# Score products of heads of 64 columns: two products on stacked rows in place of three on half rows

## The chip, the cores and the metric

The program runs on one core of one Trainium2 chip. The metric is the device time of one execution in microseconds (us). Before the change three executions took 1540.32, 1541.56 and 1544.6 us; the median, 1541.56 us, is the time before.

## The reference, cut to what matters

Two transformer blocks are computed for 256 tokens of width 1024 in fp32. The first block (latent attention, then grouped attention, each with a gated feed-forward part) isn't touched. The second block has a mixer between two feed-forward parts, and in it two kinds of attention whose heads have 64 columns:

```python
DA_HEADS = 8; DA_HEAD_DIM = 64          # differential attention: 8 heads, each of 2 components c
s = jnp.einsum('bqhcd,bkhcd->bhcqk', qblk, k) * scale
p = jax.nn.softmax(s, axis=-1)
a = p[:, :, 0] - lam * p[:, :, 1]
...
DIL_HEADS = 12; DIL_HEAD_DIM = 64       # 3 dilation groups of 4 heads each
s = jnp.einsum('nbqhd,nbkhd->nbhqk', qb, kc) * scale
s = jnp.where(valid, s, NEG)
```

A score matrix of one head component is 256 queries x 256 keys, a sum over 64 columns.

## The kernel before, in words

**Number format.** TensorE multiplies values of a rounded fp32 type (`fp32r`). To keep the accuracy of fp32, every operand is split (`split`, line 670): `hi` is the value rounded by ScalarE (`ACTIVATE`, Copy), `lo` is the value less `hi`, by VectorE (`TENSOR_TENSOR`, subtract). `mm3` (line 621) multiplies two split operands with three products into one place in PSUM: hi by hi, hi by lo, lo by hi. A product is one weight load (the queries, 128 columns) and one matmul (the keys, 256 columns).

**The mixer of the second block** (`mixer2`, line 1696). The first loop has four steps b, each with two heads. A step projects queries and keys to tokens x columns (`tm`), rotates them (`rope2`) and transposes them with TensorE into two PSUM tiles of 128 x 512: rows are head columns (component c has rows 64c to 64c+63), and the 512 columns are two heads of 256 tokens. `split` writes each PSUM tile to an `act` tile of [128, 2, 512]: plane 0 is hi, plane 1 is lo. For each head, component c and block j of 128 queries, `mm3` works on the 64 rows of the component, so on rows 0 to 63 or on rows 64 to 127: 4 x 2 x 2 x 2 = 32 scores of 128 queries, 96 products. VectorE takes the maximum, ScalarE the exponential, VectorE combines the two components, TensorE transposes the result (`pt`) and multiplies it by the values (`o`).

The second loop has two steps b for the dilated heads: three PSUM tiles pA, pB, pC (queries of groups 0 and 1, keys of groups 0 and 1, queries and keys of group 2) are split to three `act` tiles; for each slot sl (rows 64 sl on), group g and block j there is one `mm3`: 2 x 2 x 3 x 2 = 24 scores, 72 products. A fused VectorE instruction adds the mask and finds the maximum (`sm`).

**What sets the order.** No instruction runs where it is written. `record` (line 210) collects all operations, and `schedule` (line 319) orders each engine's list: six rounds of a forward pass (line 397) and a backward pass that gives each operation a latest start as its priority; the best round is kept. On TensorE the planner prices a product of `fp32r` by its output columns, whatever its rows, and knows one change of form only, that to and from outputs of 32 rows:

```python
if op.kw["lhsT"].root.dtype == F32R:
    return n / 2.4 + 13.3
```

Products into the same PSUM tile keep their written order; products of different tiles may be mixed, and projections of later steps (`tm`, `gate`) are put between them. All `act` tiles share 34 slots of SBUF, the split weights (`whi`, `wlo`) among them. The chip follows these fixed lists; each engine works through its own in order.

Of the kernel before, what the change touches and what calls it, by code (L numbers as in the profile page):

```python
# [9 lines left out]
F32 = mybir.dt.float32  # L10
F32R = mybir.dt.float32r
I32 = mybir.dt.int32
AF = mybir.ActivationFunctionType
ALU = mybir.AluOpType
# [3 lines left out]
P = 128  # L18
D = 1024
T = 256  # L20
# [526 lines left out]
class Net:  # L547
# [104 lines left out]
    def fold(self, ps, s="fold"):  # L652

        t = self.tmp(512, s)[:64]
        self.nc.scalar.activation(t, ps[64:], AF.Copy)
        self.nc.vector.tensor_tensor(t, t, ps[:64], op=ALU.add)
        return t

    def both(self, tiles, k):

        return tiles[k // 2][:, :, (k % 2) * T:(k % 2 + 1) * T]
# [1034 lines left out]
    def mixer2(self, a, rm):  # L1696
        nc = self.nc
# [16 lines left out]
        for b in range(4):  # L1714
            w = self.halves("win2a", b // 2 * 3 + b % 2)
            pts = [self.ps("qkT") for _ in range(2)]
            for j in range(2):
                ps = self.tok512(a, j, w)
                x = self.tmp(512, "qk")
                for t in range(2):  # L1720
                    nc.scalar.activation(x[:, t * T:(t + 1) * T], ps[:, t * T:(t + 1) * T], AF.Copy, scale=rqk(t, j))
                self.rope2(x, j, 8)
                for t in range(2):
                    for hd in range(2):
                        c = t * T + hd * P
                        nc.tensor.transpose(pts[t][:, hd * T + j * P:hd * T + (j + 1) * P], x[:, c:c + P], self.ident)
            qkT = []
            for pt in pts:
                o = self.act("qkT")
                self.split((o[:, 0], o[:, 1]), pt)  # L1730
                qkT.append(o)
            qT, kT = qkT
            if b % 2 == 0:
                w = self.halves("win2a", b // 2 * 3 + 2)
                vs = []
                for j in range(2):
                    o = self.act("v")
                    self.split((o[:, 0], o[:, 1]), self.tok512(a, j, w), scale=rqk(1, j))
                    vs.append(o)
            po = self.ps("o")  # L1740
            for hd in range(2):
                es = []
                for c in range(2):
                    pscore = self.ps("s")
                    c0 = c * 64
                    for j in range(2):
                        q0 = hd * T + j * P
                        self.mm3(pscore[:, j * T:(j + 1) * T],
                                 (qT[c0:c0 + 64, 0, q0:q0 + P], qT[c0:c0 + 64, 1, q0:q0 + P]),
                                 (kT[c0:c0 + 64, 0, hd * T:(hd + 1) * T], kT[c0:c0 + 64, 1, hd * T:(hd + 1) * T]),  # L1750
                                 True, True)
                    m = self.small(2)
                    nc.vector.tensor_reduce(m, pscore.rearrange("p (j n) -> p j n", j=2), axis=AX.X, op=ALU.max,
                                            negate=True)
                    e = self.tmp(512, "e")
                    l = self.small(2)
                    for j in range(2):
                        nc.scalar.activation(e[:, j * T:(j + 1) * T], pscore[:, j * T:(j + 1) * T], AF.Exp,
                                             bias=m[:, j:j + 1], accum_out=l[:, j:j + 1])
                    r = self.small(2)  # L1760
                    nc.vector.reciprocal(r, l)
                    nc.vector.tensor_scalar(r, r, (self.sig, self.siglam)[c], None, op0=ALU.mult)
                    es.append((e, r))
                (e0, r0), (e1, r1) = es
                aa = []
                for j in range(2):
                    s = slice(j * T, (j + 1) * T)
                    self.times("vector", e1[:, s], r1[:, j:j + 1])
                    nc.vector.scalar_tensor_tensor(e0[:, s], e0[:, s], r0[:, j:j + 1], e1[:, s], op0=ALU.mult,
                                                   op1=ALU.subtract)  # L1770
                    aa.append(e0[:, s])
                pT = self.transposed(aa, 2)[0]
                for c in range(2):
                    v0 = b % 2 * T + hd * P
                    self.mm3(po[:, hd * T:(hd + 1) * T], self.hl(vs[c], v0, v0 + P),
                             self.hl(pT, c * T, (c + 1) * T), c == 0, c == 1)
            os_ = self.tmp(512, "os")
            nc.scalar.activation(os_, po, AF.Copy)
            sq = self.tmp(512, "sq")
            nc.scalar.activation(sq, po, AF.Square)  # L1780
            ss = self.colsum(sq, 4)
            v = self.small(4)
            nc.vector.tensor_scalar(v, ss, 1.0 / P, self.epss, op0=ALU.mult, op1=ALU.add)
            nc.vector.tensor_scalar(v, v, 1e-37, None, op0=ALU.max)
            fit = self.small(4)
            nc.vector.tensor_scalar(fit, ss, self.ovs, self.ovt, op0=ALU.mult, op1=ALU.is_lt)
            r = self.pow_half(v, 4)
            nc.vector.tensor_tensor(r, r, fit, op=ALU.mult)
            rb = self.rows(r, 4)
            t = self.tmp(512, "on")  # L1790
            nc.vector.scalar_tensor_tensor(t, os_, self.gsub, rb, op0=ALU.mult, op1=ALU.mult)
            o = self.act("oa")
            self.split((o[:, 0], o[:, 1]), t)
            oa.append(o)
# [8 lines left out]
        for b in range(2):  # L1803
            xs, va = {}, []
            pA, pB, pC = self.ps("qT"), self.ps("kT"), self.ps("qkT")
            where = {(0, 0): (pA, 0), (0, 1): (pA, T), (0, 2): (pC, 0),
                     (1, 0): (pB, 0), (1, 1): (pB, T), (1, 2): (pC, T)}
            for t in range(2):
                w = [self.weights("win2d", (b * 3 + t) * 2 + i, 1536, 384) for i in range(2)]
                for j in range(2):  # L1810
                    ps = prod(j, w, 384)
                    x = self.tmp(384, "qk")
                    nc.scalar.activation(x, ps, AF.Copy, scale=rqk(t, j))
                    self.rope2(x, j, 6)
                    for g in range(3):
                        d, o = where[t, g]
                        nc.tensor.transpose(d[:, o + j * P:o + (j + 1) * P], x[:, g * P:(g + 1) * P], self.ident)
            tt = {}
            for p in (pA, pB, pC):
                o = self.act("qkT")  # L1820
                self.split((o[:, 0], o[:, 1]), p)
                tt[id(p)] = o
            w = [self.weights("win2d", (b * 3 + 2) * 2 + i, 1536, 384) for i in range(2)]
            for j in range(2):
                ps = prod(j, w, 384)
                o = self.act("v")
# [1 line left out]
                va.append(o)  # L1828
            po = self.ps("o")
            for sl in range(2):  # L1830
                r0 = sl * 64
                sms = [self.actf("sm")[:, :768] for _ in range(2)]
                mx = self.small(6)
                for g in range(3):
                    qd, qo = where[0, g]
                    kd, ko = where[1, g]
                    q, kk = tt[id(qd)], tt[id(kd)]
                    pscore = self.ps("s")
                    for j in range(2):
                        self.mm3(pscore[:, j * T:(j + 1) * T],  # L1840
                                 self.hl(q[r0:r0 + 64], qo + j * P, qo + (j + 1) * P),
                                 self.hl(kk[r0:r0 + 64], ko, ko + T), True, True)
                    for j in range(2):
                        nc.vector.tensor_tensor_reduce(sms[j][:, g * T:(g + 1) * T], pscore[:, j * T:(j + 1) * T],
                                                       mask[g][:, j], 1.0, NEG * 4, ALU.add, ALU.max,
                                                       mx[:, j * 3 + g:j * 3 + g + 1])
                m = self.small(2)
                nc.vector.tensor_reduce(m, mx.rearrange("p (j g) -> p j g", j=2), axis=AX.X, op=ALU.max, negate=True)
                l, r = self.small(2), self.small(2)
# [6 lines left out]
                for c in range(6):  # L1856
                    g, kc = divmod(c, 2)
# [10 lines left out]
        for i in range(8):  # L1868
            w = self.weights("win2g", i, 2048)
            g = self.gate_tile(i)  # L1870
            for mm in range(2):
                ps = self.ps("gate")
# [240 lines left out]
```

## Time and profile before

| what | value |
|---|---|
| median of three executions | 1541.56 us |
| the profiled execution | 1544.4 us, its span 1542.4 us |
| TensorE matmul (PE) | 1514.7 us busy, 98% of the span, 8808 products |
| TensorE weight load (PEld) | 1307.8 us, 85% |
| VectorE (DVE) | 1129.6 us, 73% |
| ScalarE (ACT) | 831.6 us, 54% |
| GpSimd (POOL) | 96.9 us, 6% |
| mean granted TensorE clock | 0.994 |

The profile is one execution on the chip. Busy times of matmuls include the tail of each product, so that neighbours overlap: what a product costs TensorE is read from the distance between the starts of two neighbours, not from its own duration. All operations have line 543, the line that issues the planned lists, so they are told apart by tile names: `tm` projection, `s` score, `qkT`, `qT`, `kT` transposes of queries and keys and their split, `pt` and `pT` transposed probabilities, `o` output. The two loops of the mixer lie between about 1096 and 1250 us of the span.

### The profile page before, as it was taken

The page shows a single profiled execution, that of the slowest core. Times are in us where ns is not written, and L with a number is a line of the kernel's source. Part 1 is how long each engine was busy: PE and PEld are TensorE (multiplying, and loading weights), DVE is VectorE, ACT ScalarE, POOL GpSimd, SP SyncE. Part 2 cuts the span into 40 slices and gives each one's busy share as a digit, 9 for nine tenths or more (in the row PEclk, how much of TensorE's full clock was granted, in tenths as well). Part 3 has the DMA queues.
Part 4 walks back from the last instruction along what each step waited for, and adds up shares of the span by engine and source line. Part 5 has one row for each costly group of instructions (what it writes and reads, how often), then busy time and mean ns, then how long its engine had stood idle before and what let it go on. Part 6 is the DMA issues. An engine that isn't in the chain of part 4 may idle for free.

```text
span 1542.4 us, 22782 instructions
## 1 busy us (share of the span) xinstructions
PE 1514.7 (98%) x8808; PEld 1307.8 (85%) x8808; DVE 1129.6 (73%) x2075; ACT 831.6 (54%) x1525; POOL 96.9 (6%) x109
## 2 busy tenths in 40 slices
PE   8989999999999999999999999999999999999998
PEld 6877788888788889998888888888889999888886
DVE  6478988649935757889977676765877887787752
ACT  4358944322431344786866565554756666575540
POOL 1120000000000000200000011100100000111100
PEclk8999999999999999999999999999999999999999
DMA  9355353326815731325645464454522444564450
GB/s 369 132 203 197 114 200 123 136 83 245 301 55 184 266 123 56 110 83 183 231 161 198 161 242 164 157 213 177 192 89 98 153 172 173 191 219 164 164 191 28
DMA packets 40940, 258.30 MB, mean 167 GB/s; under 512 B 4864, under 2 KB 5120, under 8 KB 14848
## 3 DMA queue, kind: packets, MB, share of 16 engines
q1 hardware_dynamic: 40832, 256.85, 46.5%
q8 instruction: 69, 1.13, 0.3%
q14 instruction: 39, 0.32, 0.1%
HBM read 255.78 MB, written 1.05 MB: 167 GB/s over the span
## 4 chain that ended last, share of the span: by engine, by line
PE 84%; DVE 7%; ACT 3%; DMA 3%; issue 2%; POOL 0%; SPq 0%; DVEq 0%; POOLq 0%; ACTq 0%
PE u L543 19%; PE g L543 19%; PE dn L543 11%; PE tm L543 10%; PE y L543 8%; PE gate L543 3%; PE s L543 2%; DVE wlo L543 2%; PE o L543 2%; PE pa L543 1%; PE p L543 1%; PE mod L543 1%; PE pt L543 1%; DVE X L543 1%; ACT whi L543 1%
## 5 line engine op out<-in xcount | busy, mean ns | idle before, releaser
L543 ACT ACTIVATE whi<-raw 128x1024 fp32r<-128x1024 f32 (+3 forms) x393 | 395.5, 1026 | 244.8 <-DMA raw<-wup 64.7
L543 DVE TENSOR_TENSOR wlo<-raw,whi 128x1024 fp32r<-128x1024 f32 (+3 forms) x393 | 458.7, 1184 | 81.6 <-PE dn L543 25.0
L543 PE MATMUL dn<-mid,whi 128*128 128x512 f32 (+1 forms) x576 | 173.4, 375 | 0.0
L543 PE MATMUL g<-h,whi 128*128 128x512 f32 (+1 forms) x528 | 170.5, 389 | 1.6 <-ACT h L543 1.1
L543 PE MATMUL u<-h,whi 128*128 128x512 f32 (+1 forms) x528 | 169.9, 388 | 0.0
L543 PE MATMUL dn<-mid,wlo 128*128 128x256 f32 (+1 forms) x376 | 122.2, 325 | 0.0
L543 PEld LDWEIGHTS dn<-mid,whi 128*128 128x128 f32 x576 | 105.2, 189 | 19.9
L543 PE MATMUL g<-a,whi 128*128 128x512 f32 x336 | 119.9, 396 | 0.4 <-DVE a L543 0.4
L543 PE MATMUL u<-a,whi 128*128 128x512 f32 x336 | 119.5, 395 | 0.0
L543 PEld LDWEIGHTS g<-h,whi 128*128 128x128 f32 x528 | 99.3, 189 | 22.2 <-ACT h L543 1.4
L543 PEld LDWEIGHTS u<-h,whi 128*128 128x128 f32 x528 | 99.6, 190 | 20.7 <-issue 0.4
L543 PE MATMUL tm<-whi,a 128*128 128x512 f32 (+1 forms) x384 | 116.5, 372 | 0.0
L543 PE MATMUL u<-h,wlo 128*128 128x256 f32 (+1 forms) x344 | 115.7, 336 | 0.0
L543 PE MATMUL g<-h,wlo 128*128 128x256 f32 (+1 forms) x344 | 115.3, 335 | 0.0
L543 PE MATMUL y<-whi,mid 128*128 128x512 f32 x352 | 109.1, 390 | 0.0
L543 PE MATMUL g<-a,wlo 128*128 128x256 f32 x336 | 94.8, 282 | 0.0
L543 PE MATMUL u<-a,wlo 128*128 128x256 f32 x336 | 94.4, 281 | 0.0
L543 POOL TENSOR_TENSOR small<-small,mhalf 128x2 f32<-128x2 f32 (+2 forms) x34 | 37.6, 1108 | 890.1 <-DVE small L543 884.4
L543 DVE SCALAR_TENSOR_TENSOR macc<-raw,sc,macc 128x1024 f32<-128x1024 f32 x70 | 86.7, 1281 | 4.8 <-DMA raw<-wmod 4.5
L543 PEld LDWEIGHTS y<-whi,mid 128*128 128x128 f32 x352 | 66.1, 188 | 13.7
L543 PEld LDWEIGHTS tm<-whi,a 128*128 128x128 f32 x384 | 70.7, 188 | 7.5
L543 PEld LDWEIGHTS dn<-mid,wlo 128*128 128x128 f32 x376 | 71.1, 189 | 6.0
(358 smaller groups left out, 3146.3 us busy)
## 6 DMA issues: line engine op xcount, KB each, us to landing
raw<-wup SPq DMA_DIRECT2D x44, 1024.0 KB, 4.7
raw<-wgu SPq DMA_DIRECT2D x44, 1024.0 KB, 4.8
raw<-wmod SPq DMA_DIRECT2D x36, 1024.0 KB, 4.9
raw<-wd SPq DMA_DIRECT2D x20, 1024.0 KB, 4.8
raw<-wdn SPq DMA_DIRECT2D x16, 1024.0 KB, 4.7
raw<-win2a SPq DMA_DIRECT2D x12, 1024.0 KB, 4.8
raw<-win2d SPq DMA_DIRECT2D x12, 768.0 KB, 4.2
wm<-wmod SPq DMA_DIRECT2D x16, 512.0 KB, 10.5
```

Of the source, the lines that this page charges most:

```text
L543: getattr(getattr(nc, op.engine), op.method)(*[res(a) for a in op.args], **{k: res(v) for k, v in op.kw.items()})
```

## The change

`stack_q` takes the place of `split` for queries, `stack_k` for keys, `mms` that of `mm3` for these scores. For component c, the queries' hi is written twice, to the component's own 64 rows and to the other 64 rows of plane c; lo goes to a tile of its own, on the component's rows. The keys' hi is written to the component's rows of plane c and lo to the other 64 rows. `mms` then makes a score with two products: one over 128 rows (hi by hi and hi by lo, added up inside the product) and one over the 64 rows of the component (lo by hi). In the second loop the third PSUM tile, which held queries and keys of group 2, is stacked with 256 columns each.

```diff
+    def stack_q(self, ps, n=512):
+        t, lo = self.act("qhh"), self.act("qlo")[:, 0, :n]
+        for c in range(2):
+            r = slice(c * 64, c * 64 + 64)
+            u = slice(64 - c * 64, 128 - c * 64)
+            nc.scalar.activation(t[r, c, :n], ps[r], AF.Copy)
+            nc.scalar.activation(t[u, c, :n], ps[r], AF.Copy)
+            nc.vector.tensor_tensor(lo[r], ps[r], t.bitcast(F32)[r, c, :n], op=ALU.subtract)
+    def stack_k(self, ps, n=512):
+        t = self.act("khl")
+        for c in range(2):
+            ...
+            nc.scalar.activation(t[r, c, :n], ps[r], AF.Copy)
+            nc.vector.tensor_tensor(t[u, c, :n], ps[r], t.bitcast(F32)[r, c, :n], op=ALU.subtract)
+    def mms(self, out, q, k, c, q0, k0):
+        r = slice(c * 64, c * 64 + 64)
+        mm(out, lhsT=t[:, c, q0:q0 + P], rhs=k[:, c, k0:k0 + T], start=True, stop=False)
+        mm(out, lhsT=lo[r, q0:q0 + P], rhs=k[r, c, k0:k0 + T], start=False, stop=True)
@@ first loop
-            for pt in pts:
-                o = self.act("qkT")
-                self.split((o[:, 0], o[:, 1]), pt)
+            qT, kT = self.stack_q(pts[0]), self.stack_k(pts[1])
-                        self.mm3(pscore[:, j * T:(j + 1) * T], ...)
+                        self.mms(pscore[:, j * T:(j + 1) * T], qT, kT, c, hd * T + j * P, hd * T)
@@ second loop
-            for p in (pA, pB, pC):
-                o = self.act("qkT")
-                self.split((o[:, 0], o[:, 1]), p)
+            qs[0] = qs[1] = self.stack_q(pA)
+            ks[0] = ks[1] = self.stack_k(pB)
+            qs[2], ks[2] = self.stack_q(pC[:, :T], T), self.stack_k(pC[:, T:], T)
-                        self.mm3(pscore[:, j * T:(j + 1) * T], ...)
+                        self.mms(pscore[:, j * T:(j + 1) * T], qs[g], ks[g], sl, g % 2 * T + j * P, g % 2 * T)
```

## Rows read from the trace of the kernel before

**Rows 1.** The page, engines: busy us, share of the span, instructions.
```profile
PE 1514.7 (98%) x8808; PEld 1307.8 (85%) x8808; DVE 1129.6 (73%) x2075; ACT 831.6 (54%) x1525; POOL 96.9 (6%) x109
```
**Rows 2.** Chain of waits, 1096 to 1250 us, shares by engine and tile.
```profile
by line: PE tm L543 62.9%; PE s L543 10.4%; PE o L543 5.5%; PE pt L543 4.4%; DVE small L543 3.5%; PE qkT L543 2.8%; PE sum L543 2.0%; DVE wlo L543 1.9%; PE gate L543 1.6%; PE rows L543 1.4%; DVE e L543 1.2%; issue 0.7%; PE kT L543 0.6%; DVE
```
**Rows 3.** Busy by window, the two loops: length; PE, PEld, DVE, ACT, POOL (instructions).
```profile
1096.00:1207.00 111.00, 110.26 (x651) 94.91 (x650) 84.66 (x202) 70.11 (x150) 4.86 (x4) 1.00 0.32 108
1207.00:1250.00 43.00, 43.00 (x288) 41.55 (x288) 35.73 (x104) 28.41 (x46) 0.00 (x0) 1.00 0.39 141
```
**Rows 4.** The same windows, score tiles alone: PE, PEld, DVE, ACT.
```profile
1096.00:1207.00 111.00, 10.12 (x100) 8.29 (x101) 10.58 (x16) 15.54 (x64) 1.00 0.32 108
1207.00:1250.00 43.00, 8.50 (x70) 7.88 (x69) 8.76 (x24) 0.00 (x0) 1.00 0.39 141
```
**Rows 5.** Timeline of PE, around a lone score product: start, us, instruction, count.
```profile
1126.45 0.40 PE L543 MATMUL tm<-wlo,a 128*128 128x512 f32 x1
1126.69 0.63 PE L543 MATMUL tm<-whi,a 128*128 128x512 f32 x2
1127.25 0.38 PE L543 MATMUL s<-qkT,qkT 64*128 64x256 f32 x1
1127.56 0.50 PE L543 MATMUL tm<-wlo,a 128*128 128x512 f32 x1
1127.89 0.63 PE L543 MATMUL tm<-whi,a 128*128 128x512 f32 x2
1128.45 1.20 PE L543 MATMUL s<-qkT,qkT 64*128 64x256 f32 x11
```
**Rows 6.** Timeline of PE, two score products and what follows.
```profile
1130.71 0.39 PE L543 MATMUL s<-qkT,qkT 64*128 64x256 f32 x2
1131.03 0.50 PE L543 MATMUL tm<-whi,a 128*128 128x512 f32 x1
1131.45 0.97 PE L543 MATMUL s<-qkT,qkT 64*128 64x256 f32 x10
```
**Rows 7.** Timeline of PE, one run of scores in the second loop.
```profile
1240.73 1.70 PE L543 MATMUL s<-qkT,qkT 64*128 64x256 f32 x12
1242.27 0.88 PE L543 MATMUL s<-qkT 64*128 64x256 f32 x6
1243.08 0.44 PE L543 MATMUL tm<-wlo,a 128*128 128x384 f32 x1
```
**Rows 8.** Timeline of PE, the longest run of the first loop.
```profile
1179.28 1.47 PE L543 MATMUL s<-qkT,qkT 64*128 64x256 f32 x20
1180.68 0.44 PE L543 MATMUL qT<-ident,qk 128*128 128x128 f32 x2
```
**Rows 9.** Timeline of PE, products of 128 rows and 256 columns.
```profile
1119.87 0.76 PE L543 MATMUL o<-pT,v 128*128 128x256 f32 x5
1120.46 0.40 PE L543 MATMUL tm<-whi,a 128*128 128x512 f32 x1
```
**Rows 10.** Timeline of the weight loads, the one of the lone score product.
```profile
1127.25 0.18 PEld L543 LDWEIGHTS s<-qkT,qkT 64*128 64x128 f32 x1 [0.37 <-issue]
```
**Rows 11.** Waits of the weight loads, 1096 to 1250 us: total us, times, longest.
```profile
PEld s L543 <- issue: 2.8, 10, 0.4
```
**Rows 12.** The split tiles of the mixer: ns min/median/max, first and last start, forms.
```profile
L543 ACT ACTIVATE qkT<-qkT x10: 589/596/603, 1102.3 to 1237.2; 128x512 fp32r<-128x512 f32 x10
L543 DVE TENSOR_TENSOR qkT<-qkT,qkT x10: 681/682/692, 1103.2 to 1238.0; 128x512 fp32r<-128x512 f32 x10
```
**Rows 13.** Split tiles elsewhere with 64 rows, and with 256 columns: the same columns.
```profile
L543 ACT ACTIVATE kT<-uk x8: 580/594/596, 119.1 to 161.9; 64x512 fp32r<-64x512 f32 x8
L543 DVE TENSOR_TENSOR kT<-uk,kT x8: 661/686/693, 120.3 to 164.2; 64x512 fp32r<-64x512 f32 x8
L543 ACT ACTIVATE kT<-kT x4: 378/392/412, 621.5 to 633.7; 128x256 fp32r<-128x256 f32 x4
L543 DVE TENSOR_TENSOR kT<-kT,kT x4: 414/418/425, 622.2 to 636.5; 128x256 fp32r<-128x256 f32 x4
```

More of the change, by code (lines that the diff above doesn't have):

```diff
@@ L657, in fold @@
         return t
+    def stack_q(self, ps, n=512):
+        nc = self.nc
+        t, lo = self.act("qhh"), self.act("qlo")[:, 0, :n]
[5 more added lines that the diff above has]
+            nc.vector.tensor_tensor(lo[r], ps[r], t.bitcast(F32)[r, c, :n], op=ALU.subtract)
+        return t, lo
+    def stack_k(self, ps, n=512):
+        nc = self.nc
+        t = self.act("khl")
+        for c in range(2):
+            r = slice(c * 64, c * 64 + 64)
+            u = slice(64 - c * 64, 128 - c * 64)
+            nc.scalar.activation(t[r, c, :n], ps[r], AF.Copy)
+            nc.vector.tensor_tensor(t[u, c, :n], ps[r], t.bitcast(F32)[r, c, :n], op=ALU.subtract)
+        return t
+    def mms(self, out, q, k, c, q0, k0):
+        mm = self.nc.tensor.matmul
+        t, lo = q
+        r = slice(c * 64, c * 64 + 64)
+        mm(out, lhsT=t[:, c, q0:q0 + P], rhs=k[:, c, k0:k0 + T], start=True, stop=False)
+        mm(out, lhsT=lo[r, q0:q0 + P], rhs=k[r, c, k0:k0 + T], start=False, stop=True)
     def both(self, tiles, k):
@@ L1726, in mixer2 @@
                         nc.tensor.transpose(pts[t][:, hd * T + j * P:hd * T + (j + 1) * P], x[:, c:c + P], self.ident)
-            qkT = []
-            for pt in pts:
-                o = self.act("qkT")
-                self.split((o[:, 0], o[:, 1]), pt)
-                qkT.append(o)
-            qT, kT = qkT
+            qT, kT = self.stack_q(pts[0]), self.stack_k(pts[1])
             if b % 2 == 0:
@@ L1744, in mixer2 @@
                     pscore = self.ps("s")
-                    c0 = c * 64
                     for j in range(2):
[L1747 to L1751, printed above, removed]
+                        self.mms(pscore[:, j * T:(j + 1) * T], qT, kT, c, hd * T + j * P, hd * T)
                     m = self.small(2)
@@ L1807, in mixer2 @@
                      (1, 0): (pB, 0), (1, 1): (pB, T), (1, 2): (pC, T)}
+            qs, ks = {}, {}
             for t in range(2):
@@ L1817, in mixer2 @@
                         nc.tensor.transpose(d[:, o + j * P:o + (j + 1) * P], x[:, g * P:(g + 1) * P], self.ident)
-            tt = {}
-            for p in (pA, pB, pC):
-                o = self.act("qkT")
-                self.split((o[:, 0], o[:, 1]), p)
-                tt[id(p)] = o
+            qs[0] = qs[1] = self.stack_q(pA)
+            ks[0] = ks[1] = self.stack_k(pB)
+            qs[2], ks[2] = self.stack_q(pC[:, :T], T), self.stack_k(pC[:, T:], T)
             w = [self.weights("win2d", (b * 3 + 2) * 2 + i, 1536, 384) for i in range(2)]
@@ L1830, in mixer2 @@
             for sl in range(2):
-                r0 = sl * 64
                 sms = [self.actf("sm")[:, :768] for _ in range(2)]
@@ L1834, in mixer2 @@
                 for g in range(3):
-                    qd, qo = where[0, g]
-                    kd, ko = where[1, g]
-                    q, kk = tt[id(qd)], tt[id(kd)]
                     pscore = self.ps("s")
                     for j in range(2):
-                        self.mm3(pscore[:, j * T:(j + 1) * T],
-                                 self.hl(q[r0:r0 + 64], qo + j * P, qo + (j + 1) * P),
-                                 self.hl(kk[r0:r0 + 64], ko, ko + T), True, True)
+                        self.mms(pscore[:, j * T:(j + 1) * T], qs[g], ks[g], sl, g % 2 * T + j * P, g % 2 * T)
                     for j in range(2):
```

## The prediction

> **What bounds the kernel now.** I read the page's engine totals first: TensorE is busy for 98% of the span [rows 1]. Then the chain of waits for the stretch of the two attention loops: `tm`, `s`, `o`, `pt` and other TensorE work carry over 90% of it; VectorE (`small`, `wlo`, `e`) has some 7%, about 10 of 154 us, in two places where probabilities are awaited [rows 2]. The busy time by window says the same: PE 153.3 of 154 us, against 120.4 for VectorE and 98.5 for ScalarE [rows 3]. So here a microsecond on TensorE is a microsecond of the end, and the other engines have room. What a score product costs TensorE is then the question, and it is read from distances between starts in the timeline.
>
> **What the scores cost now.** In a run of score products without anything between, 18 products take 1240.73 to 1243.08, 2.35 us: 0.12 us each, and 0.31 for one of them, as the lone product shows (1127.25 to 1127.56) [rows 5, 7]. A product of 128 rows and the same 256 columns takes 0.59 us for five, 0.118 [rows 9]. So 64 rows are no cheaper than 128. Two more things stand in these rows.
>
> First, going from 128 rows to 64 and back costs time. The two `tm` before the lone score take 0.56 us where their like take 0.23 to 0.24 each, so 0.10 too much; the score takes 0.31 instead of 0.12; the `tm` behind it 0.33 instead of 0.23 [rows 5]. Together 0.10 + 0.31 + 0.10 = 0.51 us for a product that costs 0.12 in a run: 0.39 for one trip to 64 rows and back. A `tm` between two such trips takes 0.42, that is 0.23 and both its 0.10s [rows 6], so the prices add up even where one product lies between. That it isn't a wait for data is seen at the load: before the lone score it stood 0.37 us, booked as "issue", waiting for nothing the profile shows, and so did ten of them, 2.8 us in all [rows 10, 11].
>
> Second, two score products on different halves of the rows can go at once: a trip with two of them took 0.32 us, no more than one [rows 6], and 20 took 1.40 us, 0.07 each, two trip ends included [rows 8].
>
> The sum before: busy time of score tiles on PE is 10.12 + 8.50 = 18.62 us [rows 4], in twelve runs by the timeline, six of which stand in [rows 5 to 8]. Busy time counts the tail of a run's last product, 0.07 us beyond the next start (1179.28 + 1.47 against 1180.68) [rows 8], so 18.62 - 12 x 0.07 = 17.8 us; with the 0.20 outside each run, 17.8 + 12 x 0.20 = 20.2 us.
>
> **What they cost after.** 56 scores (32 and 24, from the loops) have one product of 128 rows and one of 64. The first kind: 56 x 0.118 = 6.6 us. The second kind costs 0.51 for each trip, plus 0.12 for a further one in the same trip on the same half, or nothing on the other half; I take 0.06. The number of trips is not in any row, it is the planner's: products of one score tile keep their order (128, 64, 128, 64), and only when tiles are mixed do two 64s meet.
> - Tiles one after the other: 56 trips. 6.6 + 56 x 0.51 = 35.2 us, 15.0 more than now.
> - Tiles always mixed in step by two: 28 trips. 6.6 + 28 x 0.51 + 28 x 0.06 = 22.6 us, 2.4 more.
>
> Before, a run in the first loop mixes tiles (0.07 each can't come about otherwise), and the run of 18 in the second has 0.12 throughout, as on one half [rows 7, 8]. I carry that over: in the first loop 22 trips for 32 scores, since two mixed tiles out of step by one product give three trips for four scores; in the second 23 for 24. 45 trips: 6.6 + 45 x 0.51 + 11 x 0.06 = 30.2 us, **+10.0 us** against 20.2. The planner prices both kinds by columns and sees no trip, so it has no reason to bundle them: it believes that 56 products of 0.12 are saved.
>
> The Trainium skill, "TensorEngine Tiling (Array Packing)", section "Key Properties", states that changing the tiling mode, not just the tile, drains TensorE. It speaks against this change and names no price. By it alone the sum would stay open; by the rows it is 0.39 a trip, and the trace agrees in kind, since two products on different halves within the mode cost no drain [rows 6].
>
> **Splits.** An ACTIVATE of 512 columns takes 0.596 us on 128 rows [rows 12] and 0.594 on 64, a subtraction 0.682 and 0.686; with 256 columns 0.392 and 0.418 [rows 13]. First loop, per step: ScalarE from 2 to 6, VectorE from 2 to 4, all with 512 columns: + 4 x 4 x 0.594 = 9.5 us and + 4 x 2 x 0.686 = 5.5. Second loop, per step: ScalarE from 3 x 0.596 to 6 x 0.594 + 6 x 0.392, + 4.1; VectorE from 3 x 0.682 to 4 x 0.686 + 4 x 0.418, + 2.4; twice that. In all + 17.7 us on ScalarE and + 10.3 on VectorE, in a stretch where they are idle for 55.5 and 33.6 us [rows 3]. Their cover is `tm` of later steps on TensorE. Without cover, the time from the transposes to the first score grows, but component 0 needs only half of the new splits. Where VectorE leads already (about 10 us, [rows 2]) extra work is late at once. Bounds: the new VectorE work wholly exposed, + 10.3; below, - 2, since component 0 no longer waits for component 1 and TensorE's longer scores leave others more time. I take + 1, near the low end, because PE has hardly any idle time in either window.
>
> The new tiles take three `act` slots per step of the first loop where two were held, and six where three were in the second; a weight split that finds no slot would come later. With 0.7 us of idle PE in 154 [rows 3] I price that at nothing, at most at the + 10.3 already taken as an end. DMA queues get nothing new.
>
> Sum: + 10.0 + 1 = + 11 us on the profiled execution, 1544.4 to 1555.4. That execution lies 2.8 above the median shown, so 1552.5.
>
> **Rivals.**
> - *Trips are bundled* (28 or fewer): + 2.4 + 1, so 1545. For it: the first loop does mix tiles in step in its last run [rows 8]. Against it: the second loop doesn't [rows 7]. Fewer than 20 trips would be needed for no loss: 6.6 + 20 x 0.51 + 36 x 0.06 = 19.0, - 1.2.
> - *Trips cost nothing, and a third of the products goes* (the other side). If what I price as trips is in truth the wait for the splits that happen to come before each run, alternating is free. Then the scores cost 56 x 2 x 0.118 = 13.2 us, 7.0 less than now, + 1 for the splits: 1535.5. It would decide from under about 0.13 us a trip: 13.2 + 56 x 0.13 = 20.5. Against it: the `tm` behind a lone score waits for no score, and takes 0.10 more all the same [rows 5]. The Trainium skill, "TensorE: Matmul & The Clock Gate", Part 2, states that TensorE pulls a weight load ahead of running products; by that the load ahead of a 64-row product is hidden, as this rival wants. The trace disagrees at these places [rows 10].
> - *The splits set the pace.* VectorE's + 10.3 is exposed on top of the trips: + 10.0 + 10.3, so 1562. For it: VectorE is 78% busy here. Against it: TensorE has `tm` to do meanwhile.
> - *The change isn't what it says.* If other scores were still made of three products nothing would move; but both loops call the new function, so this has no chance worth a number.
>
> **Chances.** A difference of about 0.3%, 4.6 us, can be told from no change. Forecast (35 to 56 trips, splits mostly covered, 1548 to 1558): 0.62. Bundled: 0.19, mostly within 0.3%. Free trips: 0.08. Splits exposed: 0.11. The range runs from 1543 to 1560; it leaves out the free trips, the best of the bundled and half of the exposed splits. Slower by over 0.3% (over 1546.2): 0.78; within: 0.15; faster: 0.07.
>
> **What would show it.** Right: the timeline of PE with `s` of 128 rows and of 64 rows in turn, 45 or so separate visits to 64 rows, a weight load before each that stands about 0.37 us on "issue"; score time with its edges at 30 us; the end later by as much. 112 score products. ScalarE + 18 and VectorE + 10 us busy, with PE still idle for under 2 us in the loops. Wrong: 64-row products of 0.12 between 128-row ones; fewer than 28 trips; PE idle for several us before the first score of a step, with VectorE as the releaser.

## The result and the profile after

The changed kernel takes 1577.32 us (median of four, 1573.96 to 1579.56) against 1540.94 for the kernel before beside it: ratio 1.0229, 95% interval 1.0204 to 1.0254, 35 to 36 us slower. The forecast was 1552.5, in 1543 to 1560: the direction was right, the size was more than three times the 11 us forecast.

The profiled execution of the changed kernel took 1573.96 us, with a span of 1571.8. On its page TensorE is as busy as before (98%, [rows 1]), with 56 products fewer; the other engines have gained 12 and 17 us:

```profile
PE 1543.3 (98%) x8752; PEld 1323.7 (84%) x8752; DVE 1141.5 (73%) x2093; ACT 848.5 (54%) x1559; POOL 96.3 (6%) x109
```

Where the time came from is seen in the starts of common instructions. The first product of the mixer into `rows` (from `rm`) starts at 1087.7 us before and 1084.3 after, the last gate product at 1297.4 and 1324.6: the stretch of the two loops and the gates has grown from 209.7 to 240.3 us, by **30.6**. Ahead of it the new plan is 3.4 us shorter, behind it 2.2 longer. Busy time by window, after (length, then PE, PEld, DVE, ACT, POOL, then the mean granted clock; the windows are first loop, second loop, gates), to be held against [rows 3]:

```profile
1093.00:1204.00 111.00, 110.12 (x519) 89.08 (x518) 79.31 (x186) 69.70 (x152) 3.12 (x3) 0.92 0.25 86
1204.00:1273.00 69.00, 67.77 (x350) 59.16 (x349) 48.33 (x128) 43.50 (x75) 1.07 (x1) 0.90 0.30 107
1273.00:1325.00 52.00, 52.00 (x307) 45.71 (x307) 42.92 (x72) 34.42 (x55) 0.00 (x0) 0.97 0.57 202
```

TensorE has no idle time to speak of, 2 us in 180; yet the granted clock, 1.00 in both loops before, is 0.92, 0.90 and 0.97. The score tiles alone, against [rows 4], and the forms of their products (ns min/median/max):

```profile
1093.00:1204.00 111.00, 19.32 (x64) 11.50 (x64) 10.68 (x16) 15.47 (x64) 0.92 0.25 86
1204.00:1273.00 69.00, 17.89 (x48) 10.47 (x48) 8.77 (x23) 0.00 (x0) 0.90 0.30 107
```
```profile
L543 PE MATMUL s<-khl,qhh x56: 276/384/581, 1104.2 to 1271.6; 128*128 128x256 f32 x56
L543 PE MATMUL s<-khl,qlo x56: 378/381/579, 1104.5 to 1272.1; 64*128 64x256 f32 x56
```

A third of the products is gone and their busy time has doubled, from 18.6 to 37.2 us. The timeline of PE shows two reasons. With the clock full (1104 to 1107 us), the two forms follow each other every 0.31 us, and nothing else stands between; the later rows are at a fallen clock:

```profile
1104.22 0.38 PE L543 MATMUL s<-khl,qhh 128*128 128x256 f32 x1 [0.79 <-DVE khl L543]
1104.53 0.38 PE L543 MATMUL s<-khl,qlo 64*128 64x256 f32 x1
1104.84 0.39 PE L543 MATMUL s<-khl,qhh 128*128 128x256 f32 x1
1105.16 0.38 PE L543 MATMUL s<-khl,qlo 64*128 64x256 f32 x1
...
1167.91 1.05 PE L543 MATMUL tm<-whi,a 128*128 128x512 f32 x2
1168.77 0.63 PE L543 MATMUL tm<-wlo,a 128*128 128x512 f32 x1
...
1170.31 0.63 PE L543 MATMUL tm<-whi,a 128*128 128x512 f32 x2
1170.78 0.39 PE L543 MATMUL tm<-wlo,a 128*128 128x512 f32 x1
...
1226.29 0.58 PE L543 MATMUL s<-khl,qhh 128*128 128x256 f32 x1
1226.80 0.58 PE L543 MATMUL s<-khl,qlo 64*128 64x256 f32 x1
1227.31 0.58 PE L543 MATMUL s<-khl,qhh 128*128 128x256 f32 x1
```

A score takes 0.62 us, as the rows of before had promised (0.118 + 0.51). In the rows from 1226.29 the same sequence takes 0.51 a product, and the projections behind another run of scores take 0.43 (two from 1167.91 to 1168.77) where they take 0.235 two microseconds later. The granted clock is 0.50 from 1164 to 1170 us and from 1228 to 1234, and 1.00 from 1170.2 to 1172: where products are slow, it is at the lower of its two levels, 1.2 in place of 2.4 GHz. It falls in the course of a run of scores or right behind it, as behind the eight from 1104.22 to 1108.7 us; in the two windows below no score runs (columns as above):

```profile
1110.00:1112.00 2.00, 2.00 (x6) 1.52 (x6) 2.00 (x4) 2.00 (x10) 0.00 (x0) 0.50 0.01 4
1112.00:1120.00 8.00, 8.00 (x41) 6.55 (x40) 5.42 (x20) 4.16 (x7) 0.00 (x0) 1.00 0.39 133
```

### The profile page after: what moved, and what is told of

Its sections match the earlier page's. It is cut to its first block, busy times and chain, and to the rows that moved or that the text cites. A ratio compares the mean times of both kernels' runs of the same rounds, so it can differ in the third digit from the quotient of the medians.

```text
span 1571.8 us, 22730 instructions
## 1 busy us (share of the span) xinstructions
PE 1543.3 (98%) x8752; PEld 1323.7 (84%) x8752; DVE 1141.5 (73%) x2093; ACT 848.5 (54%) x1559; POOL 96.3 (6%) x109
## 4 chain that ended last, share of the span: by engine, by line
PE 85%; DVE 7%; ACT 3%; DMA 2%; issue 2%; POOL 0%; SPq 0%; DVEq 0%; POOLq 0%; ACTq 0%
PE u L543 19%; PE g L543 19%; PE dn L543 12%; PE tm L543 10%; PE y L543 8%; PE s L543 3%; PE gate L543 3%; DVE wlo L543 2%; PE pa L543 1%; PE o L543 1%; PE p L543 1%; PE mod L543 1%; PE pt L543 1%; DVE X L543 1%; PE uq L543 1%
## 5 line engine op out<-in xcount | busy, mean ns | idle before, releaser
L543 PE MATMUL tm<-whi,a 128*128 128x512 f32 (+1 forms) x384 | 122.1, 391 | 0.0
L543 PEld LDWEIGHTS tm<-whi,a 128*128 128x128 f32 x384 | 75.8, 202 | 8.7 <-issue 0.4
L543 PEld LDWEIGHTS u<-a,whi 128*128 128x128 f32 x336 | 63.1, 188 | 15.4
```

What stands on the lines that cost most here:

```text
L543: getattr(getattr(nc, op.engine), op.method)(*[res(a) for a in op.args], **{k: res(v) for k, v in op.kw.items()})
```

## The experiments

Each kernel ran beside the kernel before on the same chip; ratios are to that. Diffs are cut to the lines that matter; `...` marks a cut.

**No 64-row product at all.** lo of the queries is stacked twice too.

```diff
-        t, lo = self.act("qhh"), self.act("qlo")[:, 0, :n]
+        t, lo = self.act("qhh"), self.act("qll")
...
-            nc.vector.tensor_tensor(lo[r], ps[r], t.bitcast(F32)[r, c, :n], op=ALU.subtract)
+            nc.vector.tensor_tensor(lo[r, c, :n], ps[r], t.bitcast(F32)[r, c, :n], op=ALU.subtract)
+            nc.vector.tensor_tensor(lo[u, c, :n], ps[r], t.bitcast(F32)[r, c, :n], op=ALU.subtract)
...
-        mm(out, lhsT=lo[r, q0:q0 + P], rhs=k[r, c, k0:k0 + T], start=False, stop=True)
+        mm(out, lhsT=lo[:, c, q0:q0 + P], rhs=k[:, c, k0:k0 + T], start=False, stop=True)
```

> The changed kernel, but lo of the queries is written twice as well, so that the second product also goes over 128 rows (it adds lo by lo, a term that was left out before). No product of a score has 64 rows, so there is no change of row form; VectorE has two more subtractions per stack of queries. Trips and clock (my theory: each visit to 64 rows costs about 0.4 us, and many of them in a row let TensorE's clock fall): scores cost 112 x 0.118 = 13.2 us where the kernel before has 20.2, granted clock 1.00 in both loops, about 1533 to 1537 us. Splits and slots (rival: the longer splitting, the extra act tiles and the new plan are what costs): they are all still here and larger, so over 1565 us.

Measured: 1554.68 us, ratio 1.0070 (1.0047 to 1.0092). Some 24 us of the 35 are gone with the 64-row products, against the rival; but it is not faster than before, against my theory. Clock and scores did what I expected (1.00; 16.2 us busy). The rest is idle TensorE, 9.4 of 157 us. The window of both loops, and what PE and, in the last row, PEld waited for from 1093 to 1262 us (total us, times, longest):

```profile
1093.00:1250.00 157.00, 147.63 (x877) 133.15 (x876) 132.22 (x317) 109.82 (x221) 4.82 (x5) 1.00 0.31 108
```
```profile
PE pt L543 <- DVE sm L543: 4.9, 2, 2.7
PE s L543 <- DVE khl L543: 4.4, 4, 1.5
PE pt L543 <- DVE e L543: 1.5, 1, 1.5
PE o L543 <- DVE pT L543: 1.0, 2, 0.6
PEld s L543 <- ACT whi L543: 4.2, 3, 1.8
```

PE's own waits are for VectorE, though loads of score weights waited 4.2 us for ScalarE. VectorE is busy for 1146.8 us of the span, 17 more than before, so it may set the pace at places; the experiment with the copy below tries that.

**Fewer visits to 64 rows, the same products.** The products of one score tile, and then of all tiles of a head or slot, are held together, first those of 128 rows and then those of 64.

```diff
...
+        for out, (t, lo), k, c, q0, k0 in jobs:
+            mm(out, lhsT=t[:, c, q0:q0 + P], rhs=k[:, c, k0:k0 + T], start=..., stop=False)
...
+        for i, (out, (t, lo), k, c, q0, k0) in enumerate(jobs):
+            r = slice(c * 64, c * 64 + 64)
+            mm(out, lhsT=lo[r, q0:q0 + P], rhs=k[r, c, k0:k0 + T], start=False, stop=...)
+        self.nc.together(first)
```

> The changed kernel with the four products of a score tile held together on TensorE in the order 128, 128, 64, 64 rows: 28 visits to 64 rows instead of 54. Trips and clock: 6.6 + 28 x 0.51 + 28 x 0.12 = 24.3 us of scores, 4 more than before, and at most half of the 17 us that the fallen clock costs: 1545 to 1554 us. Trips alone (rival: the clock is no separate cause, each trip simply costs 0.70 us, (31 + 7) / 54): 28 x 0.70 - 7 = + 12.6, 1554 us, with the clock as low as after. Splits and slots: over 1565 us.

> The same for all score tiles of a head (first loop: four products of 128 rows, then four of 64 with the components in turn) or of a slot (second loop: six, then six): 12 visits to 64 rows. Trips and clock: 6.6 + 8 x 0.63 + 4 x 1.11 = 16.1 us of scores, 4 less than before, clock 1.00: 1536 to 1540 us. Trips alone at 0.70: 12 x 0.70 - 7 = + 1.4, 1542 us. Splits and slots: over 1565 us.

Measured: by tile (28 visits) 1549.23 us, ratio 1.0039 (1.0024 to 1.0054); by head (12 visits) 1543.7 us, ratio 0.9997 (0.9981 to 1.0013). Score tiles by tile; then, by head, the timeline of PE for the two heads of a step, and both loops:

```profile
1093.00:1250.00 157.00, 23.86 (x112) 17.20 (x112) 17.36 (x36) 15.11 (x64) 1.00 0.31 110
```
```profile
1104.26 0.63 PE L543 MATMUL s<-khl,qhh 128*128 128x256 f32 x4
1104.82 0.50 PE L543 MATMUL s<-khl,qlo 64*128 64x256 f32 x4
1105.25 0.74 PE L543 MATMUL s<-khl,qhh 128*128 128x256 f32 x4
1105.92 0.50 PE L543 MATMUL s<-khl,qlo 64*128 64x256 f32 x4
```
```profile
1093.00:1184.00 91.00, 89.96 (x498) 75.61 (x497) 74.37 (x170) 65.36 (x146) 3.02 (x3) 1.00 0.31 106
1184.00:1244.00 60.00, 58.89 (x375) 55.77 (x375) 50.45 (x138) 44.41 (x78) 1.01 (x1) 1.00 0.35 123
```

54, 28 and 12 visits give 37.2, 23.9 and 16.0 us of busy score time ([rows 4] have 18.6), and the loss falls from 2.29% to 0.39% and to nothing: the same products and the same splits, so neither the splits nor the plan's slots are the main cause. With 28 visits the clock is 1.00 in the profiled execution, as my theory allowed and "trips alone" didn't. By head the time is 4 to 8 us above what I wrote (the kernel before was 3 us slower on that chip as well), though the scores are 2.6 us shorter than before: TensorE idles for 2.1 us in 151, and the splits are the next suspect.

**The clock by itself.** All visits stay, and each score gets two products of 128 rows that its own first product overwrites.

```diff
+        for _ in range(2):
+            mm(out, lhsT=t[:, c, q0:q0 + P], rhs=k[:, c, k0:k0 + T], start=True, stop=True)
         mm(out, lhsT=t[:, c, q0:q0 + P], rhs=k[:, c, k0:k0 + T], start=True, stop=False)
```

> The changed kernel with two products more ahead of each score, over 128 rows, whose result the score overwrites: 112 x 0.118 = 13.2 us of work that does nothing, with all the visits to 64 rows kept. Trips and clock: the visits are further apart, the granted clock in the loops rises from about 0.91 towards 1.00, and the extra work pays for itself: 1570 to 1580 us. Trips alone, or splits and slots: 13 us longer than the changed kernel, 1590 us.

Measured: 1573.09 us, ratio 1.0194 (1.0170 to 1.0219): 13.2 us of work are added to the changed kernel, and it takes 0.35% (5.4 us) less time. The two intervals overlap, so that it is shorter isn't shown; that the work came at no cost is, for 1590 us was the forecast without the clock. Windows of the loops and gates, and the score tiles in the two loops:

```profile
1093.00:1204.00 111.00, 110.32 (x579) 90.56 (x578) 81.58 (x186) 71.02 (x151) 3.02 (x3) 1.00 0.27 90
1204.00:1273.00 69.00, 68.97 (x405) 61.79 (x405) 50.00 (x134) 42.97 (x75) 1.01 (x1) 1.00 0.29 104
1273.00:1325.00 52.00, 52.00 (x318) 45.96 (x318) 44.04 (x70) 36.35 (x57) 0.00 (x0) 1.00 0.58 205
```
```profile
1093.00:1204.00 111.00, 27.29 (x128) 19.58 (x128) 11.02 (x16) 16.10 (x64) 1.00 0.27 90
1204.00:1273.00 69.00, 20.48 (x96) 14.62 (x96) 8.38 (x23) 0.00 (x0) 1.00 0.29 104
```

56 visits, and the clock stays at 1.00. Less the filler, the scores are 47.8 - 13.2 = 34.6 us busy at full clock: 16 more than before. What came back is the clock's part: 13.2 + 5.4 = 18.6 us by the ratios. By the profiles it is 15.2: here the stretch from the first `rows` product (1084.9) to the last gate product (1323.2) takes 238.3 us, less the filler 225.1, which is 15.4 of the 30.6 us above before. The granted clocks of the changed kernel's three windows lie between the two, if the work in them goes as the clock does: 0.08 x 111 + 0.10 x 69 + 0.03 x 52 = 17.3 us (an estimate). So the clock costs 15 to 19 us.

**The parts by loop.** The change in one loop, the code before in the other; for the second loop alone:

```diff
-            qT, kT = self.stack_q(pts[0]), self.stack_k(pts[1])
+            qkT = []
+            for pt in pts:
+                o = self.act("qkT")
+                self.split((o[:, 0], o[:, 1]), pt)
+                qkT.append(o)
+            qT, kT = qkT
...
```

> The change in the first loop alone. Trips and clock: about 32 visits x 0.51 + 32 x 0.118 - 10.7 = + 9.4 us, and half of the clock's 17 us: + 8.5; about 1559 us, with the granted clock at 1.00 in the second loop. Splits and slots: + 2 to + 6, since the first loop adds only 5.5 us of VectorE work.

> The change in the second loop alone. Trips and clock: about 22 visits x 0.51 + 24 x 0.118 - 9.4 = + 4.7 us, and half of the clock's 17 us: + 8.5; about 1555 us, with the granted clock at 1.00 in the first loop. The sum of both parts should come to the whole, + 36 us, less what each plan does elsewhere. Splits and slots: + 5 or less.

Measured: first loop alone 1560.26 us, ratio 1.0100 (1.0083 to 1.0117); second alone 1557.42 us, ratio 1.0083 (1.0064 to 1.0101). First and second loop by window, for the one and for the other:

```profile
1093.00:1204.00 111.00, 110.17 (x517) 88.97 (x516) 79.15 (x185) 69.64 (x152) 3.12 (x3) 0.92 0.26 89
1204.00:1262.00 58.00, 58.00 (x385) 56.25 (x384) 46.71 (x130) 36.67 (x59) 1.01 (x1) 1.00 0.41 146
```
```profile
1093.00:1204.00 111.00, 110.27 (x649) 94.72 (x648) 85.68 (x214) 71.80 (x159) 4.83 (x5) 1.00 0.32 111
1204.00:1262.00 58.00, 58.00 (x278) 48.85 (x277) 40.57 (x113) 36.11 (x62) 0.00 (x0) 0.85 0.28 100
```

Both times are near the forecast by trips and clock (1559 and 1555) and far from that by splits. The clock falls in the loop that has the change and not in the other. From the same two starts as above, the stretch has grown by 15.9 and by 14.7 us, 30.6 together, as much as in the changed kernel. That they fit so well is in part luck of the executions: by medians the parts are 15.6 and 12.7, 28 of 36 us, and the profiled execution of the second loop alone was the longest of its four (1562.33).

**The splits by themselves.** Before's products, and beside them the added split work, written to a tile that nobody reads.

```diff
...
+            self.extra(pts[0], 4, 2)          # first loop: ACTIVATEs, subtractions
...
+            self.extra(pA, 3, 1)
+            self.extra(pB, 4, 3)              # second loop
```

> The kernel before, with its three products of 64 rows, and beside them the split work that the change adds: 4 ACTIVATEs and 2 subtractions of 512 columns in each step of the first loop, 7 and 4 in each step of the second, into a tile that nobody reads. If splits are hidden while TensorE is the bound: 0 to + 3 us. If the splits set the pace by themselves (as the idle TensorE in the kernel without 64-row products could mean): + 6 to + 12 us.

Measured: 1551.31 us, ratio 1.0035 (1.0021 to 1.0049), + 5.4 us (6.6 by the medians): near the lower end of what the theory says that I didn't hold. PE idles 5.2 of 162 us in the window of the loops:

```profile
1093.00:1255.00 162.00, 156.81 (x950) 138.45 (x949) 131.44 (x322) 112.64 (x229) 4.74 (x5) 1.00 0.34 121
```

**Whose time it is without 64-row products.** The second writing of lo goes from VectorE to ScalarE; the diff is to the kernel without any 64-row product.

```diff
-            nc.vector.tensor_tensor(lo[u, c, :n], ps[r], t.bitcast(F32)[r, c, :n], op=ALU.subtract)
+            nc.scalar.activation(lo[u, c, :n], lo.bitcast(F32)[r, c, :n], AF.Copy)
```

> The kernel without any 64-row score product, but with the second writing of the queries' lo as a copy by ScalarE in place of a subtraction by VectorE: 9.9 us less VectorE work, 10 us more on ScalarE. If VectorE sets the pace there (it is busy for 143.5 of 169 us and TensorE idles for 12): 5 to 10 us shorter than with the subtraction, 1545 to 1550 us. Rival: it is the longer chain from the transposes to the first score that costs, whoever does it; the copy makes it longer by a hop, so no shorter, 1553 us or more.

Measured: 1548.25 us, ratio 1.0012 (0.9997 to 1.0026), 9 us below the 1.0070 of the subtraction, as forecast if VectorE sets the pace. VectorE falls from 132.2 to 127.2 us in the same window and idle PE from 9.4 to 5.1, although the chain has a hop more:

```profile
1093.00:1250.00 157.00, 151.91 (x893) 136.07 (x893) 127.16 (x319) 121.05 (x242) 4.83 (x5) 1.00 0.33 114
```

**Pairs on both halves.** The kernel before, with the products of the two components (or slots) held together and in turn; then with all four tiles of a step of the first loop together.

```diff
...
+        for pair in rows:
+            for n, (a, b) in enumerate(((0, 0), (0, 1), (1, 0))):
+                for out, l, r in pair:
+                    mm(out, lhsT=l[a], rhs=r[b], start=n == 0, stop=n == 2)
+        self.nc.together(first)
...
```

> The kernel before (three products of 64 rows a score, splits as before), with the products of the two components of a head, or of the two slots of a group, held together on TensorE and in turn, so that neighbours lie on different halves of the rows. 84 pairs x 0.12 + 14 visits x 0.39 = 15.5 us of scores where the kernel before has 20.2. If pairs on different halves go at once and TensorE is the bound: 4 to 5 us faster than before, about 1537 us. Rival: holding two score tiles together delays VectorE and ScalarE by as much, no change or slower.

> The kernel before with paired products, and in the first loop the four score tiles of a step held together: 4 visits to 64 rows there instead of 8. 4 x 0.39 = 1.6 us shorter than with pairs by head, about 1538 us. Rival: four tiles at once let VectorE and ScalarE wait longer and hold four of the eight PSUM tiles: 1541 us or more.

Measured: 1539.36 us, ratio 0.9967 (0.9954 to 0.9979); with four tiles 1540.7 us, ratio 0.9970 (0.9954 to 0.9986). Twelve products take 0.90 us, in the timeline of the first; below, its score tiles:

```profile
1104.53 0.97 PE L543 MATMUL s<-qkT,qkT 64*128 64x256 f32 x12
1105.43 0.74 PE L543 MATMUL tm<-whi,a 128*128 128x512 f32 x2
```
```profile
1093.00:1250.00 157.00, 12.63 (x168) 10.60 (x168) 19.04 (x40) 15.49 (x64) 0.99 0.34 120
```

168 products in 12.6 us busy, where 112 of the changed kernel's take 37.2 (34.6 at full clock). The first of these versions is 5 us faster than the kernel before. The further 1.6 us of larger groups can't be told from nothing.

## Why the prediction was wrong, point by point

- **TensorE bounds the loops: right.** It idles for 2 us in 180 after, and the stretch is longer by what its products cost.
- **A visit to 64 rows costs 0.51 us, 0.39 above a product: right in size.** A score in turn takes 0.62 us at full clock; 28 and 12 visits come out at 23.9 and 16.0 us busy (which leaves out the 0.2 us at the edges of each run) against 24.3 and 16.1 expected. The weight loads wait on "issue" as foreseen, though by 0.2 us at most (waits of the weight loads in the two loops of the changed kernel, total us, times, longest):

```profile
PEld s L543 <- issue: 5.4, 25, 0.2
```

  The rival "trips cost nothing" is refuted.
- **45 visits: too few.** There are 54: 24 for the 24 scores of the second loop, near the 23 assumed, but 30 for the 32 of the first in place of 22. I carried the mixing of tiles over from the kernel before, but the new plan runs nearly tile after tile; only two visits hold two 64-row products (1106.53 and 1191.55 us). By the prediction's own prices 54 visits make 6.6 + 54 x 0.51 + 2 x 0.06 - 20.2 = + 14.1 us in place of + 10.0, and the filler's stretch has + 15.4 at full clock, splits included.
- **No term for the clock: this is the step that failed.** Every price was taken at the clock of before, 1.00 [rows 3], and held constant, without a word on why it should hold. With runs of products that come every 0.31 us, 0.39 of each score's 0.62 us in changes of row form, the granted clock fell to 0.92 and 0.90 on the mean, and what came behind, projections of other steps too, ran at 1.2 GHz for a while. That is 15 to 19 us, about half of the whole, where the sum had nothing. It is not a price of its own per visit: 56 visits with more work between leave the clock at 1.00, and so, in the profiled execution, do 28 visits with two scores each, made of the same products in another order. The profile of before could not show it, but it showed PE "busy" through tails, so that 98% busy says nothing of pauses between products. The Trainium skill, "TensorE: Matmul & The Clock Gate", section "A second HAM failure mode: psum-queue depth-cycling", describes a kernel whose matmuls pause briefly between groups, often enough for the clock to go back and forth between its levels. The trace agrees that the clock can go back and forth while the profile shows TensorE busy for 178 of 180 us; here it goes with changes of row form, which that section doesn't name, and that it is their pauses which let it fall is argued, not shown.
- **Splits + 1 us: right here, though not safely.** The work came as priced (ScalarE + 17 us, VectorE + 12), and idle PE in the loops rose from 0.7 to 2.1 us. The same work beside the products of before cost 5 to 7 us, midway between + 1 and the bound of + 10.3. That the slow scores gave cover in the changed kernel is argued, not shown: by head, with faster scores, TensorE idles for 2.1 us too.
- **The sum.** + 15 for scores and splits at full clock and + 15 to 19 for the clock make 30 to 34, where the stretch of the profiled pair has 30.6. The medians lie 36 apart: the four executions of the changed kernel had mean clocks of 0.984, 0.983, 0.979 and 0.979 over the span, and the profiled one was the shortest (1573.96), while the profiled one of the kernel before (1544.4) lies 3 above its median. That the direction was right owes nothing to the term that failed: the visits were seen, and they alone make it slower.

What stays open: how close the visits must lie for the clock to fall. The runs show 54 close together (it falls), 56 with two more products between (it doesn't) and 28 (it doesn't in the profiled execution, the fastest of ten; the ten had means of 0.989 to 0.996, where the kernel before beside them had 0.992 to 0.996). Nor does a run part the pauses from whatever else comes with a visit.

## What to carry to other kernels

Counting products is not enough where they differ in rows: look in the timeline for what a lone product of another row form costs with its neighbours, and multiply by the visits, not by the products. A sum of TensorE prices holds only at the clock at which they were read; if a change puts short pauses into a stretch that had none, price the stretch at the lower level as an end of the range. Two products of heads of 64 columns that go in turn on both halves cost together what one product of 128 rows costs (0.12 us: twelve take 0.90, and 0.19 of it is what the first product of a visit takes above one in a run), and ordering them so was worth more here than removing products.

## What the runs showed of the hardware that was not expected

- Work that does nothing can cost nothing: 13.2 us of filler products brought 15 to 19 us back, with the granted clock from 0.92 and 0.90 to 1.00 in the two loops.
- Two 64-row products on different halves of the rows cost 0.15 us together when six pairs run at a time (twelve in 0.90 us; the 0.10 us on either side of a visit not counted), against 0.12 for one alone in a long run [rows 7].
- A subtraction or copy of 64 rows costs as much as one of 128 [rows 12, 13], so stacking multiplies split work: it put 29 us more onto ScalarE and VectorE here (17 and 12). Though TensorE was busy for nearly all of the two loops before [rows 3], 5 to 7 us came to the end when that work was added beside its products.
